# Streamed high and low parts in one tile, in pieces of 64 or 128 bytes, and another order in one down projection

## The chip, the cores and the metric

The kernel runs on one core of a Trainium2 chip. The metric is device microseconds of one execution. TensorE has two levels of clock, 1.2 and 2.4 GHz; the profile shows the granted share of the higher one.

## The reference

Two blocks run one after the other on 256 tokens of width 1024, each of two layers, and what they compute is float32. The first block's layers have four branches (a convolution, a sparse attention, a chunked linear recurrence and a memory attention) and a feed forward. The second block's layers are modulated: a vector `c` gives shift, scale and gate for each half of a layer. Its layer 0 mixes with two chunked recurrences, its layer 1 with a long convolution. Both end in the feed forward that the change touches:

```
h = h + g2 * swiglu(modulate(h, norm2_w[i], sh2, sc2), ffn_w1[i], ffn_w3[i], ffn_w2[i])
swiglu(u, w1, w3, w2) = (silu(u @ w1) * (u @ w3)) @ w2          # 1024 -> 2816 -> 1024
modulate(x, gain, shift, scale) = rmsnorm(x, gain) * (1 + scale) + shift
```

A last norm follows.

## The kernel before

Activations lie transposed: channels on the 128 partitions, `KT` = 8 tiles of channels, and the 256 tokens along the row. A product in float32 accuracy is made of three matmuls in the format float32r: the weights `w` are split into a high part `wh` and what is left over, `wl`, and so is the streamed operand (`xh` and `xl`, in other stages `hh` and `hl`, `ph` and `pl`, `ydh` and `ydl`). `mm3` (lines 486 to 490) issues high by high, then high weights by the low operand, then low weights by the high operand, all into one place of PSUM. The weights are the stationary operand, 128x128 at a time; the activations are streamed, 256 columns.

`weights` (line 458) brings a unit of four tiles of rows by 256 columns, 512 KB, by a DMA on SP's queue; ScalarE writes `wh` (line 474), VectorE writes `wl` (line 475). There are 4 buffers of `w` and 3 each of `wh` and `wl`. A unit feeds 24 matmuls: 4 row tiles, 2 halves of 128 columns, 3 products. `s_tiles` (line 492) runs through the row tiles for one output of 2 x 128 channels by 256 tokens.

`ffn` (line 540) loops over 11 blocks of 256 hidden channels: a gate product and an up product, SiLU on ScalarE, a multiplication on VectorE, and `split` (line 455) into `ph` and `pl`, two tiles of 22 rows of 256 floats. Then come four down projections over the 22 rows, and `residual` adds them to `xT`. `ffn2` (line 1984) prepares it in the second block: `ahead` and `ffn_ahead` run the first hidden block on a not yet normalised copy (`uh`, `ul`), while `norm_split` (line 437) writes `xh` and `xl`, two tiles of 8 rows of 256 floats under the tags `hh` and `hl` of the layer's pool. In layer 0 the tiles `uh` and `ul` lie at the other end of SBUF than in layer 1. The order of the work on each engine is that of the program text. The first block calls `ffn` as well, without `gcol`.

Of the kernel before, what the change touches and what calls it, by code (L numbers as in the profile page):

```python
# [11 lines left out]
F32R = mybir.dt.float32r  # L12
# [7 lines left out]
S = 256  # L20
KT = 8
# [4 lines left out]
FT = FFN // 128  # L26
# [212 lines left out]
class Halves:  # L239


    def __init__(self, *tiles):
        self.tiles = tiles

    def __getitem__(self, i):
        return self.tiles[i[1] // 4][i[0], i[1] % 4, i[2]]


class Ahead:
    def __init__(self, h, l, n, pb, lp):  # L250
        self.h, self.l, self.n, self.pb, self.lp = h, l, n, pb, lp
# [2 lines left out]
class K:  # L254
    def __init__(self, tc, A, out, tap=None):
        self.tc, self.nc, self.A, self.out, self.tap_ = tc, tc.nc, A, out, tap
        self.es = ExitStack()
        self.bank, self.mmbank = "aux", "mm"
        self.held = None
        self.bg, self.rate, self.due, self.has_modc, self.fg = None, 0.0, 0.0, False, iter(())  # L260
        es = self.es
        self.const = es.enter_context(tc.tile_pool(name="const", bufs=1))
        self.xp = es.enter_context(tc.tile_pool(name="xp", bufs=1))
        self.wp = es.enter_context(tc.tile_pool(name="wp", bufs=2))
        self.wpool, self.wb = self.wp, WB
        self.ps = es.enter_context(tc.tile_pool(name="ps", bufs=4, space=bass.MemoryType.PSUM))
        self.wk = es.enter_context(tc.tile_pool(name="wk", bufs=2))
        self.dr = es.enter_context(tc.tile_pool(name="dr", bufs=1, space=bass.MemoryType.DRAM))
# [168 lines left out]
    def norm_split(self, src, g, hh, hl, shift=None, r=None, bank="aux2", u=None):  # L437
        nc = self.nc
        pb = u.pb if u else self.rstd_bcast(src, r, bank)
        for k in range(KT):  # L440
            t = self.wk.tile([128, S], F32, tag="nt", bufs=3, name="nt")
            nc.vector.scalar_tensor_tensor(t, src[:, k, :], g[:, k:k + 1], pb, op0=OP.mult, op1=OP.mult)
            if shift is None:
                nc.scalar.copy(hh[:, k, :], t)
                nc.vector.tensor_tensor(hl[:, k, :], t, hh[:, k, :], OP.subtract)
            else:
                nc.scalar.activation(hh[:, k, :], t, AF.Identity, bias=shift[:, k:k + 1])
                nc.vector.scalar_tensor_tensor(hl[:, k, :], t, shift[:, k:k + 1], hh[:, k, :], op0=OP.add,
                                               op1=OP.subtract)
# [3 lines left out]
        self.nc.vector.scalar_tensor_tensor(lo, src, g, hi, op0=OP.mult, op1=OP.subtract)  # L453

    def split(self, src, hi, lo):
        self.nc.scalar.copy(hi, src)
        self.nc.vector.tensor_tensor(lo, src, hi, OP.subtract)

# [26 lines left out]

    def mm3(self, ps, wh, wl, xh, xl, start, stop):
        nc = self.nc
        nc.tensor.matmul(ps, wh, xh, start=start, stop=False)  # L488
        nc.tensor.matmul(ps, wh, xl, start=False, stop=False)  # L489
        nc.tensor.matmul(ps, wl, xh, start=False, stop=stop)  # L490

    def s_tiles(self, ps, at, xh, xl, kt=KT, first=True, last=True, x0=0, mws=((0, 128), (128, 128)), k0=0):

        for n in range(kt):
            k = (n + k0) % kt
            wh, wl = at(k)
            st, sp = first and n == 0, last and n == kt - 1  # L500
            for i, (m0, mw) in enumerate(mws):
                self.mm3(ps[:mw, i * S:(i + 1) * S], wh[:, m0:m0 + mw], wl[:, m0:m0 + mw], xh[:, x0 + k, :],
                         xl[:, x0 + k, :], st and i == 0, sp and i == len(mws) - 1)

    def s_form(self, name, l, c0, ncols, xh, xl, kt=KT, k0=0):
# [31 lines left out]
        nc.vector.tensor_tensor(pr, pg, pu, OP.mult)  # L537
        return pr

    def ffn(self, xh, xl, l, w_gate, w_up, u0, w_down, gcol=None, first=None, scale=None):  # L540
        nc = self.nc
        with self.pool("ffn") as fp:
            ph = fp.tile([128, FT, S], F32R, name="ph")
            pl = fp.tile([128, FT, S], F32R, name="pl")
            for i in range(FFN // 256):
                self.pump()
                if i == 0 and first is not None:
                    prv = first
                else:
                    pg = self.mm()  # L550
                    self.s_tiles(pg, self.weights(w_gate, l, i * 256), xh, xl)
                    pu = self.mm()
                    self.s_tiles(pu, self.weights(w_up, l, u0 + i * 256), xh, xl)
                    sg = fp.tile([128, 512], F32, tag="f1", bufs=2, name="f1")
                    pr = fp.tile([128, 512], F32, tag="f2", bufs=2, name="f2")
                    if scale is not None:
                        for o, ps in ((sg, pg), (pr, pu)):
                            nc.vector.tensor_tensor(o.rearrange("p (m t) -> p m t", m=2),
                                                    ps.rearrange("p (m t) -> p m t", m=2),
                                                    scale[:, None, :].to_broadcast([128, 2, S]), OP.mult)  # L560
                        pg, pu = sg, pr
                    nc.scalar.activation(sg, pg, AF.Silu)
                    nc.vector.tensor_tensor(pr, sg, pu, OP.mult)
                    prv = pr.rearrange("p (m t) -> p m t", m=2)
                self.split(prv, ph[:, 2 * i:2 * i + 2, :], pl[:, 2 * i:2 * i + 2, :])
            self.rate = RATES[4]
            for i in range(4):
                self.pump()
                pd = self.mm()
                self.s_tiles(pd, self.weights(w_down, l, i * 256, FT), ph, pl, FT)  # L570
                for m in range(2):
                    self.residual(2 * i + m, pd[:, m * S:(m + 1) * S], gcol)

    def residual(self, k, ps, gcol=None):
        nc = self.nc
        if gcol is None:
            nc.vector.tensor_tensor(self.xT[:, k, :], self.xT[:, k, :], ps, OP.add)
        else:
            nc.vector.scalar_tensor_tensor(self.xT[:, k, :], ps, gcol[:, k:k + 1], self.xT[:, k, :], op0=OP.mult,
                                           op1=OP.add)  # L580
# [1402 lines left out]

    def ffn2(self, i, hp, fp=None):
        A = self.A
        xh = hp.tile([128, KT, S], F32R, tag="hh", name="xh")
        xl = hp.tile([128, KT, S], F32R, tag="hl", name="xl")
        g, sh = self.gains[:, 2 * i + 1, :], self.mod[i][:, 24:32]
        with self.pool("f2") as lp:
            with self.pool("f2u", None if i else "right") as up:  # L1990
                u = self.ahead(self.xT, g, up, sh)
                self.norm_ahead(u, self.xT)
                pr = self.ffn_ahead(u, i, "ffn_w1_2", "ffn_w3_2", 0, lp)
                self.norm_split(self.xT, g, xh, xl, shift=sh, u=u)
            self.fill(9, "aux2")
            if fp:
                self.dft_loads()
            self.ffn(xh, xl, i, "ffn_w1_2", "ffn_w3_2", 0, "ffn_w2_2", gcol=self.mod[i][:, 40:48], first=pr)
        self.tap(f"hl{i}", self.xT)


# [280 lines left out]
```

## Time and profile before

| | us |
|---|---|
| median of 3 runs | 2015.56 (2011.5 to 2017.99) |
| the profiled execution | 2005.55 |
| its span, first to last instruction | 2003.8 |
| PE busy | 1950.2 |
| DVE busy | 1487.3 |
| ACT busy | 1049.6 |
| mean granted clock of TensorE | 0.981 |

PE is TensorE's matmuls and PEld its weight loads; DVE is VectorE, ACT ScalarE, SP the engine that issues the DMAs. The length of a matmul in the profile is from its start to its modelled end; matmuls follow one another before the one in front has ended, so the distance of two starts, and not the length, is what one costs. The count of a stretch holds every instruction that lies in it, if only in part, so a stretch of 25 us with matmuls of 0.28 us holds the starts of 25.28 us.

### The profile page before, as it was taken

To read this page: it belongs to the slowest core of one execution; us is meant where nothing else is said; L and a number is where in the kernel's file an instruction comes from. 1 tells how busy PE (TensorE), PEld (TensorE's weight loads), DVE (VectorE), ACT (ScalarE), POOL (GpSimd) and SP (SyncE) were. 2 spreads that over 40 slices of the span, in tenths; PEclk is the share of its full clock that TensorE was granted. 3 is DMA by queue.
4 is the path that set the end of the run, shared out by engine and by line. 5 is a ranking of instruction groups with operands and counts; after the bars stand their busy time and mean duration, and the time that the engine had idled before them with its cause. 6 is when DMAs were issued, how large, how long until landed. Compare 5 with 4: busy or idle time off the path is not lost.

```text
span 2003.8 us, 39753 instructions
## 1 busy us (share of the span) xinstructions
PE 1950.2 (97%) x16274; PEld 1889.9 (94%) x16274; DVE 1487.3 (74%) x2374; ACT 1049.6 (52%) x1640; POOL 96.4 (5%) x86
## 2 busy tenths in 40 slices
PE   8999999999999999999979999999999999999998
PEld 8999999999999999999969999998899999999998
DVE  5988877796776879968657775777776556897554
ACT  6663454675544673454544544645345445656443
POOL 0001000010000000000100000000020000001001
PEclk9999999999999999999987999989999999999999
DMA  8865756875667756748523456534246666546663
GB/s 317 280 217 170 232 179 209 292 256 192 205 221 242 244 188 220 242 129 288 180 89 101 153 166 192 175 99 124 85 124 181 192 189 219 162 126 187 192 188 126
DMA packets 118558, 379.55 MB, mean 189 GB/s; under 512 B 18239, under 2 KB 28776, under 8 KB 117096
## 3 DMA queue, kind: packets, MB, share of 16 engines
q1 hardware_dynamic: 118376, 377.02, 58.2%
q8 instruction: 127, 2.08, 0.4%
q14 instruction: 55, 0.45, 0.1%
HBM read 366.53 MB, written 10.25 MB: 188 GB/s over the span
## 4 chain that ended last, share of the span: by engine, by line
PE 88%; DVE 4%; ACT 3%; issue 2%; DMA 2%; POOL 0%; SPq 0%; DVEq 0%; POOLq 0%; ACTq 0%
PE mm L490 23%; PE mm L488 23%; PE mm L489 23%; DVE wl L475 2%; ACT wh L474 1%; PE aux L1230 1%; PE mm L524 1%; PE mm L525 1%; PE mm L526 1%; PE mm L2080 1%; PE aux L2132 1%; PE aux L490 1%; PE aux L2115 1%; PE aux L861 1%; PE aux L488 1%
## 5 line engine op out<-in xcount | busy, mean ns | idle before, releaser
L474 ACT CAST wh<-w 128x1024 fp32r<-128x1024 f32 (+2 forms) x570 | 588.9, 1035 | 644.7 <-PE mm L489 485.3
L475 DVE TENSOR_TENSOR wl<-w,wh 128x1024 fp32r<-128x1024 f32 (+2 forms) x570 | 684.6, 1203 | 302.1 <-ACT wh L474 298.6
L488 PE MATMUL mm<-hh,wh 128*128 128x256 f32 x1776 | 502.7, 283 | 2.3 <-ACT bq L768 2.0
L490 PE MATMUL mm<-hh,wl 128*128 128x256 f32 (+1 forms) x1776 | 503.0, 283 | 1.1 <-DVE wl L475 1.1
L489 PE MATMUL mm<-hl,wh 128*128 128x256 f32 x1776 | 501.2, 282 | 0.0
L488 PEld LDWEIGHTS mm<-hh,wh 128*128 128x128 f32 x1776 | 335.2, 189 | 6.1 <-ACT bq L768 2.4
L490 PEld LDWEIGHTS mm<-hh,wl 128*128 128x128 f32 (+1 forms) x1776 | 334.9, 189 | 3.7 <-issue 1.5
L489 PEld LDWEIGHTS mm<-hl,wh 128*128 128x128 f32 x1776 | 335.1, 189 | 3.0 <-issue 2.3
L490 PE MATMUL mm<-xh,wl 128*128 128x256 f32 x960 | 270.6, 283 | 1.6 <-DVE wl L475 1.5
L488 PE MATMUL mm<-xh,wh 128*128 128x256 f32 x960 | 269.4, 282 | 2.1 <-DVE dqT L1268 1.1
L489 PE MATMUL mm<-xl,wh 128*128 128x256 f32 x960 | 269.6, 283 | 0.2
L490 PE MATMUL mm<-ph,wl 128*128 128x256 f32 x704 | 196.1, 279 | 0.0
L488 PE MATMUL mm<-ph,wh 128*128 128x256 f32 x704 | 195.8, 278 | 0.0
L489 PE MATMUL mm<-pl,wh 128*128 128x256 f32 x704 | 195.7, 278 | 0.0
L488 PEld LDWEIGHTS mm<-xh,wh 128*128 128x128 f32 x960 | 182.4, 190 | 6.1 <-issue 2.9
L490 PEld LDWEIGHTS mm<-xh,wl 128*128 128x128 f32 x960 | 182.7, 190 | 5.6 <-issue 3.0
L489 PEld LDWEIGHTS mm<-xl,wh 128*128 128x128 f32 x960 | 182.2, 190 | 2.9 <-issue 2.2
L1224 DVE SCALAR_TENSOR_TENSOR macc<-mw,cs,macc 128x512 f32<-128x512 f32 x196 | 145.5, 747 | 11.9 <-DMA mw<-in_t_mod_w 11.4
L489 PEld LDWEIGHTS mm<-pl,wh 128*128 128x128 f32 x704 | 132.4, 188 | 0.0
L490 PEld LDWEIGHTS mm<-ph,wl 128*128 128x128 f32 x704 | 132.1, 188 | 0.0
L488 PEld LDWEIGHTS mm<-ph,wh 128*128 128x128 f32 x704 | 132.0, 188 | 0.0
L488 PE MATMUL mm<-brh,wh 128*128 128x256 f32 x384 | 107.8, 281 | 0.0
(702 smaller groups left out, 3518.7 us busy)
## 6 DMA issues: line engine op xcount, KB each, us to landing
w<-in_t_w_in SPq DMA_DIRECT2D x148, 512.0 KB, 4.2
w<-in_t_ffn_w SPq DMA_DIRECT2D x128, 512.0 KB, 3.7
mw<-in_t_mod_w SPq DMA_DIRECT2D x96, 512.0 KB, 4.8
w<-in_t_ffn_w_up SPq DMA_DIRECT2D x88, 512.0 KB, 3.5
w<-in_t_ab_w_in SPq DMA_DIRECT2D x42, 512.0 KB, 3.4
w<-in_t_ffn_w_down SPq DMA_DIRECT2D x40, 512.0 KB, 3.6
w<-in_t_w_lift SPq DMA_DIRECT2D x32, 512.0 KB, 3.9
w<-in_t_hy_w_in SPq DMA_DIRECT2D x24, 512.0 KB, 3.7
```

Of the source, the lines that this page charges most:

```text
L474: nc.scalar.copy(wh, w)
L475: nc.vector.tensor_tensor(wl, w, wh, OP.subtract)
L488: nc.tensor.matmul(ps, wh, xh, start=start, stop=False)
L489: nc.tensor.matmul(ps, wh, xl, start=False, stop=False)
L490: nc.tensor.matmul(ps, wl, xh, start=False, stop=stop)
L524: nc.tensor.matmul(o, h, wh, start=(k + tb == 0), stop=False)
L525: nc.tensor.matmul(o, h, wl, start=False, stop=False)
L526: nc.tensor.matmul(o, l, wh, start=False, stop=(k == KT - 1 and tb == 1))
L861: nc.tensor.matmul(ps[:, jj * S:jj * S + ns], qr[r, 2 * jp + jj, tb * 128:(tb + 1) * 128], kr[r, 0, :ns], start=True, stop=True)
L1224: nc.vector.scalar_tensor_tensor(acc, v[:, k, :], sc, acc, op0=OP.mult, op1=OP.add)
L1230: nc.tensor.matmul(ps[:, m:m + 1], acc[:, m * 128:(m + 1) * 128], self.ones[:, :1], start=True, stop=True)
L2080: nc.tensor.matmul(ps[:, i * 256:(i + 1) * 256], self.Hm[:, (2 * j + i) * 128:(2 * j + i + 1) * 128], t[:, j, :], start=True, stop=True)
```

## The change

The second block's feed forwards get one tile `xx` in place of `xh` and `xl`. In each of its 8 rows the high and the low part take turns in pieces: 16 floats (64 bytes) in layer 0, 32 floats (128 bytes) in layer 1. A view, `Lines`, picks the high or the low pieces, so that a matmul streams 256 floats as 16 pieces with a step of 128 bytes, or as 8 pieces with a step of 256. `like` gives the other operands of an instruction the same shape. In layer 1 `ph` and `pl` share a tile `pp` in the same way, in pieces of 64 bytes. In layer 0 they stay two tiles, and the three matmuls of a step of the down projection come in another order: low weights by the high operand, then high by high, then high weights by the low operand. `xx` is a tile of the pool `f2`, not of the layer's pool.

```diff
+class Lines:
+    def __init__(self, tile, j):
+        self.tile, self.j = tile, j
+
+    def __getitem__(self, i):
+        return self.tile[i[0], i[1], :, self.j, :]
+
+def like(src, dst):
+    if len(dst.shape) == len(src.shape):
+        return src
+    lead = "p m" if len(src.shape) == 3 else "p"
+    return src.rearrange(f"{lead} (a b) -> {lead} a b", b=dst.shape[-1])
...
@@ norm_split, with a shift
+                t = like(t, hh[:, k, :])
@@ split
+        src = like(src, hi)
@@ mm3
-        nc.tensor.matmul(ps, wh, xh, start=start, stop=False)
-        nc.tensor.matmul(ps, wh, xl, start=False, stop=False)
-        nc.tensor.matmul(ps, wl, xh, start=False, stop=stop)
+        order = [(wl, xh), (wh, xh), (wh, xl)] if self.low_first else [(wh, xh), (wh, xl), (wl, xh)]
+        for i, (w, x) in enumerate(order):
+            nc.tensor.matmul(ps, w, x, start=start and i == 0, stop=stop and i == 2)
@@ s_tiles
+                h = xh[:, x0 + k, :]
+                self.mm3(like(ps[:mw, i * S:(i + 1) * S], h), wh[:, m0:m0 + mw], wl[:, m0:m0 + mw], h,
@@ ffn(..., lines=None)
+            if lines:
+                pp = fp.tile([128, FT, S // lines, 2, lines], F32R, name="pp")
+                ph, pl = Lines(pp, 0), Lines(pp, 1)
...
+            self.low_first = gcol is not None and not lines
             for i in range(4):
...
+            self.low_first = False
@@ ffn2
-        xh = hp.tile([128, KT, S], F32R, tag="hh", name="xh")
-        xl = hp.tile([128, KT, S], F32R, tag="hl", name="xl")
...
+            xx = lp.tile([128, KT, 8 if i else 16, 2, 32 if i else 16], F32R, name="xx")
+            xh, xl = Lines(xx, 0), Lines(xx, 1)
...
+            self.ffn(xh, xl, i, "ffn_w1_2", "ffn_w3_2", 0, "ffn_w2_2", gcol=self.mod[i][:, 40:48], first=pr,
+                     lines=16 if i else None)
```

## Rows read from the trace of the kernel before

**Rows 1.** The page's head: busy time by engine, and shares of the chain.
```profile
PE 1950.2 (97%) x16274; PEld 1889.9 (94%) x16274; DVE 1487.3 (74%) x2374; ACT 1049.6 (52%) x1640; POOL 96.4 (5%) x86
...
PE 88%; DVE 4%; ACT 3%; issue 2%; DMA 2%; POOL 0%; SPq 0%; DVEq 0%; POOLq 0%; ACTq 0%
PE mm L490 23%; PE mm L488 23%; PE mm L489 23%; DVE wl L475 2%; ACT wh L474 1%; PE aux L1230 1%; PE mm L524 1%; PE mm L525 1%; PE mm L526 1%; PE mm L2080 1%; PE aux L2132 1%; PE aux L490 1%; PE aux L2115 1%; PE aux L861 1%; PE aux L488 1%
```
**Rows 2.** Stretches: PE, PEld, DVE, ACT, POOL busy (count); clock, DMA share, GB/s.
```profile
1200.00:1225.00 25.00, 25.00 (x215) 25.00 (x214) 13.97 (x16) 10.75 (x14) 0.82 (x1) 1.00 0.66 211
...
1575.00:1600.00 25.00, 25.00 (x223) 25.00 (x222) 14.30 (x15) 12.02 (x15) 0.00 (x0) 1.00 0.69 193
...
1950.00:1975.00 25.00, 25.00 (x219) 25.00 (x218) 13.31 (x16) 10.36 (x12) 2.85 (x3) 1.00 0.64 201
```
**Rows 3.** Order of time, PE, layer 0's gate and up: start us, length.
```profile
1559.73 0.28 PE L488 MATMUL mm<-xh,wh 128*128 128x256 f32 x1
...
1560.07 0.28 PE L488 MATMUL mm<-xh,wh 128*128 128x256 f32 x1
1560.18 0.28 PE L489 MATMUL mm<-xl,wh 128*128 128x256 f32 x1
...
1562.79 0.28 PE L488 MATMUL mm<-xh,wh 128*128 128x256 f32 x1
```
**Rows 4.** Order of time, PE, first block's feed forward.
```profile
560.02 0.28 PE L488 MATMUL mm<-hh,wh 128*128 128x256 f32 x1
...
562.85 0.28 PE L488 MATMUL mm<-hh,wh 128*128 128x256 f32 x1
```
**Rows 5.** Order of time, PE, layer 0's output projection.
```profile
1490.81 0.28 PE L488 MATMUL mm<-ydh,wh 128*128 128x256 f32 x1
...
1493.31 0.28 PE L488 MATMUL mm<-ydh,wh 128*128 128x256 f32 x1
```
**Rows 6.** Order of time, PE, first block, another stage.
```profile
354.60 0.28 PE L488 MATMUL mm<-hh,wh 128*128 128x256 f32 x1
...
357.32 0.28 PE L488 MATMUL mm<-hh,wh 128*128 128x256 f32 x1
```
**Rows 7.** Order of time, PE, layer 1's down projection.
```profile
1965.12 0.28 PE L488 MATMUL mm<-ph,wh 128*128 128x256 f32 x1
...
1967.95 0.28 PE L488 MATMUL mm<-ph,wh 128*128 128x256 f32 x1
```
**Rows 8.** Order of time, weight loads, the stretch of rows 3.
```profile
1560.07 0.19 PEld L489 LDWEIGHTS mm<-xl,wh 128*128 128x128 f32 x1
```
**Rows 9.** Order of time, matmuls and weight loads with shorter streams, merged.
```profile
1729.45 3.29 PE L2132 MATMUL aux<-G,hy 128*128 128x128 f32 x28
...
197.71 0.74 PEld L1230 LDWEIGHTS aux<-cst,macc 128*128 128x128 f32 x6
```
**Rows 10.** Groups, 1505 to 1690 us: busy us, mean ns, idle before them.
```profile
L489 PE MATMUL mm<-xl,wh 128*128 128x256 f32 x320 | 87.9, 276 | 0.0
L474 ACT CAST wh<-w 128x1024 fp32r<-128x1024 f32 (+1 forms) x68 | 69.7, 1027 | 85.5 <-PE mm L489 68.1 <-issue 16.8 <-ACT sq L366 0.4
L490 PEld LDWEIGHTS mm<-xh,wl 128*128 128x128 f32 x320 | 60.1, 188 | 0.4 <-DVE wl L475 0.3
L490 PE MATMUL mm<-ph,wl 128*128 128x256 f32 x176 | 48.6, 276 | 0.0
```
**Rows 11.** Order of time, transposes, merged.
```profile
1734.47 0.60 PE L2106 MATMUL aux<-cst,hsd 128*128 128x128 f32 x4
```
**Rows 12.** Lines 1724 and 1725: least, median, greatest ns, starts, forms.
```profile
L1724 PE MATMUL aux<-dX,dG x256: 219/219/293, 1126.5 to 1396.3; 64*64 64x32 f32 x128
...
L1725 ACT COPY dT<-aux x8: 353/372/372, 1129.9 to 1396.7; 128x256 f32<-128x256 f32 x8
```
**Rows 13.** Tile xh, 1505 to 1690 us: the same columns, then who waited.
```profile
L447 ACT ACTIVATE xh<-nt,mod x8: 492/500/513, 1507.2 to 1518.2; 128x256 fp32r<-128x256 f32 x8
...
  PEld mm L488: 0.3, 1
```

More of the change, by code (lines that the diff above doesn't have):

```diff
@@ L258, in __init__ @@
         self.bank, self.mmbank = "aux", "mm"
-        self.held = None
+        self.held, self.low_first = None, False
         self.bg, self.rate, self.due, self.has_modc, self.fg = None, 0.0, 0.0, False, iter(())
@@ L501, in s_tiles @@
             for i, (m0, mw) in enumerate(mws):
-                self.mm3(ps[:mw, i * S:(i + 1) * S], wh[:, m0:m0 + mw], wl[:, m0:m0 + mw], xh[:, x0 + k, :],
+                h = xh[:, x0 + k, :]
+                self.mm3(like(ps[:mw, i * S:(i + 1) * S], h), wh[:, m0:m0 + mw], wl[:, m0:m0 + mw], h,
                          xl[:, x0 + k, :], st and i == 0, sp and i == len(mws) - 1)
@@ L538, in ffn_ahead, with ffn @@
         return pr
-    def ffn(self, xh, xl, l, w_gate, w_up, u0, w_down, gcol=None, first=None, scale=None):
+    def ffn(self, xh, xl, l, w_gate, w_up, u0, w_down, gcol=None, first=None, scale=None, lines=None):
         nc = self.nc
         with self.pool("ffn") as fp:
-            ph = fp.tile([128, FT, S], F32R, name="ph")
-            pl = fp.tile([128, FT, S], F32R, name="pl")
+            if lines:
+                pp = fp.tile([128, FT, S // lines, 2, lines], F32R, name="pp")
+                ph, pl = Lines(pp, 0), Lines(pp, 1)
+            else:
+                ph = fp.tile([128, FT, S], F32R, name="ph")
+                pl = fp.tile([128, FT, S], F32R, name="pl")
             for i in range(FFN // 256):
@@ L1997, in ffn2 @@
                 self.dft_loads()
-            self.ffn(xh, xl, i, "ffn_w1_2", "ffn_w3_2", 0, "ffn_w2_2", gcol=self.mod[i][:, 40:48], first=pr)
+            self.ffn(xh, xl, i, "ffn_w1_2", "ffn_w3_2", 0, "ffn_w2_2", gcol=self.mod[i][:, 40:48], first=pr,
+                     lines=16 if i else None)
         self.tap(f"hl{i}", self.xT)
```

## The prediction

> **What bounds the kernel now.** I read the head of the page first. TensorE is busy for 1950.2 of 2003.8 us, and the chain of waits that ended last is 88% PE; its three largest shares are the three matmul lines of `mm3` [rows 1]. So the end is set by how often a matmul can start, and a changed wait on another engine matters only where it leaves a gap on PE. The second view is the table of stretches [rows 2], for the stages that the diff touches: layer 0's second feed forward (about 1510 to 1680 us) and layer 1's (about 1822 to 1993). PE is busy in all of each 25 us there, at a granted clock of 1.00: nothing to win from waits, nor from the clock. What differs is the count: 223 matmuls in a stretch of these stages, 215 in the first block's feed forward at the same busy share and clock.
>
> The third view, the order of time, shows why. In layer 0's gate and up part, 27 matmuls lie between the starts at 1559.73 and 1562.79: 113.3 ns each [rows 3]. In the first block 24 lie between 560.02 and 562.85: 117.9 ns each [rows 4]. With operand `ydh` 21 lie between 1490.81 and 1493.31: 119.0 ns [rows 5]. The shape is the same in all three, 256 fp32 columns against 128x128 weights. What differs is where the streamed tile lies. By the program's own addresses each weight row starts 128 bytes behind a multiple of 256; `xh`, `xl` and the second block's `ph`, `pl` start 64 behind one, `hh` and `hl` 192, `ydh` 128, just where the weights do. So the price of a matmul hangs on the streamed tile's place against the weights, and that is what the change moves. It is not place alone: `hh` at its usual place also ran at 113.3 ns for a while (24 from 354.60 to 357.32 [rows 6]), and `ph` of layer 1, usually at 113.3, slipped to 117.9 (24 from 1965.12 to 1967.95 [rows 7]). There are levels, and a stage can fall from one to another; the stretch with the slip counts 219 instead of 223 [rows 2].
>
> What the time goes into: a weight load starts just behind a matmul, and the next matmul only when that load is through (a matmul at 1560.07, the load for the next at 1560.07 too, the next at 1560.18 [rows 3, 8]). The loop is a loop of weight loads. Matmuls with a stream half as long and weights as wide give its floor: 28 in 3.29 us, less 0.27 for the last one's own length, are 27 intervals of 111.9 ns; six weight loads whose matmuls stream one column take 0.74 us, less 0.19, five of 110 ns [rows 9]. Against 111.9 the stages lose 1.4 ns a matmul now, which I read as the two reads of SBUF getting in each other's way. This reading is a theory; no row shows a bank.
>
> A rule of the Trainium skill speaks against it and against the change: "SBUF — State Buffer", section "A bandwidth-pool intuition that's wrong", gives the weight load a second, independent read port, so a stream's layout should cost nothing. By that the sum would be 0. The trace disagrees with it: 113.3, 117.9 and 119.0 ns for one shape.
>
> **The change part by part.**
>
> Gate and up, both layers: 10 pairs of tiles at 2 x 8 x 2 x 3 = 96 matmuls are 960 in each layer (three lines with 320 [rows 10]). The streamed row becomes pieces of 64 bytes (layer 0) or 128 (layer 1), high and low in turn. The count of matmuls stays. The second down projection (3 x 176 = 528) gets pieces of 64. Together 2448 matmuls stream pieces. What one costs then no row shows, as no matmul of 256 columns streams pieces. Below: 111.9 ns, the loop of weight loads [rows 9], gains 1.4 x 2448 = 3.4 us. Lower still: transposes, where four in 0.60 us less 0.27 are 109 to 110 ns each [rows 11], would gain 4.0 x 2448 = 9.8 us. Above: 119.0 ns [rows 5] loses 5.7 x 2448 = 14.0 us. I take 111.9: each part now touches only every other piece of a line, so the weights' row meets it in half of its places, and the nearest rows for a load with little in its way are those of rows 9. That is a gain of 3.4 us.
>
> That pieces in themselves cost no stream time is bounded by one row: line 1724's matmuls stream two pieces of 16 elements in one half of the calls and 32 in one run in the other, and all 256 have 219 ns as least and median [rows 12]. This is a tile of 32 columns, too short to show a nanosecond a piece; 16 pieces at 1 ns would give 16 ns on a stream, and nothing covers this but the few ns by which the weight loads are longer. It belongs to the slow end.
>
> The slip in layer 1's down projection [rows 7] costs 4 matmuls of 113.3 ns in its stretch, 219 for 223 [rows 2], or 0.45 us; with what falls into the next stretch, which holds the kernel's end too, I put it at 0.6 us. If the new layout does not slip, that goes. If both down projections slipped throughout, 1056 x 4.5 = 4.8 us would come. I take the gain of 0.6.
>
> Low weights first, layer 0's down projection (528 matmuls, tiles plain as before): the three matmuls of a step are the same three, and each load still runs beside a stream at the same distance: high beside weights twice, low once. I cost it at nothing. Two covers are needed. The first matmul of a unit now waits for `wl` (DVE) where it waited for `wh` (ACT). In steady state both are written more than a unit ahead: ACT's casts wait 68.1 us in all for PE to give back a buffer, and PE waits 0.3 us for `wl` over that feed forward [rows 10]. And `wh` is given back by the third matmul and not by the second, 0.11 us later; 22 units x 0.11 = 2.5 us if ACT had no such idle time. Bounds: -0.8 us (528 at 111.9) to +2.5.
>
> Writing in pieces: 8 ACT instructions of 500 ns [rows 13] and as many of DVE's write a layer's `xx`, 10 or 11 of each kind write `pp`. The nearest row is an ACT copy of 128x256 that writes runs of 16 or 32 floats, 353 to 372 ns [rows 12]; no penalty is seen. The pieces matter where PE waits for the norm: 0.3 us for `xh` [rows 13]. If each of these 16 were 0.1 us longer and all on the path, both layers would lose 3.2 us; I take 0.
>
> Moved tiles: `xx` is a tile of its own below `f0`, 16 KB, so `ph` moves by 16 KB: the same place modulo 256 for the plain pair of layer 0. No DMA, no queue and no instruction before 1490 us moves, so the weights arrive as before; the DMA engines are 0.64 to 0.69 busy in these stretches [rows 2].
>
> **Sum.** -3.4 - 0.6 = -4.0 us on the profiled execution of 2005.55 (span 2003.8, 1.75 us around it): 2001.5. That execution lies 10 us below the median of the three runs, 2015.56, and below the lowest of them, 2011.5; I take the difference over to the median: 2011.5.
>
> **The rivals.**
>
> B, the loads too get out of the way: the loop falls below the 111.9 ns, to the 109.3 of the transposes [rows 11]; -9.8 - 0.6, 2005.2. For it: the weights in a transpose are 128 wide too. Against it: no plain matmul in the rows goes below 111.9 in a long run. The Trainium skill has a rule that would give this: "TensorE: Matmul & The Clock Gate", section "Back-to-back issue gap", estimates 256/2.4 + 2.5 = 109.2 ns; by it 4.1 x 2448 = 10.0 us would go. The trace's long runs of this shape do not show it.
>
> C, nothing happens: the level of 113.3 is the same for pieces, since half as many meetings that last twice as long cost the same; 2015.6. For it: three tiles at the same place, `xh` and `ph` of both layers, all have 113.3 whatever lies beside them. Against it: the level does respond to place.
>
> D, slower: in 64-byte pieces the low part starts 64 bytes behind the high, at 128 modulo 256, just where the weights start, as `ydh` does now. Where the start decides, the low matmuls go to 119.0: a third of 960 + 528, 496 x 5.7 = 2.8 us; in 128-byte pieces the low part starts at 192, the place of `hh`: 320 x 4.6 = 1.5. That is +4.3, 2019.9. It decides as soon as place of start, and not the run of lines, sets the level. If the whole triple falls with its low member, which is how the slips look (all three at 117.9), it is 1488 x 5.7 + 960 x 4.6 = +12.9, 2028.5. For it: rows 4 and 5 are just these places. Against it: rows 6, the same place at 113.3.
>
> **How the numbers follow.** About 0.3% (6 us) is what a measurement of this kernel can tell from no change. Chances: the forecast 0.48, B 0.19, C 0.14, D 0.19. The forecast's own range is 2006 to 2017, by run-to-run spread and by the bounds of low-first and of the slips. Faster by over 0.3%, below 2009.5: nearly all of B (0.18) and two fifths of the forecast (0.20), 0.38. Slower, above 2021.6: most of D, 0.17. Within: the rest, 0.45. The range runs from 2001, B with its spread, to 2023, which takes in D by starts alone and leaves its worse form out.
>
> **What would show it.** Right: 226 or so matmuls in a stretch of gate and up (25.28 us, with the ends, by 111.9 ns), both layers alike; 223 still in layer 0's down projection; no 219 in layer 1's. B shows 230. C shows 223 everywhere. D shows 215 to 219 with pieces, and layer 0, with 64 bytes, worse than layer 1. Writing in pieces shows as longer ACT and DVE rows for `xx` and more PE idle ahead of the first tile. The prediction is wrong if the stretches keep their count, or if the total moves by much more than 2448 times the change of one interval.

## The result, and the profile after

The changed kernel is slower by half a per cent: a ratio of 1.0051, with a 95% interval of 1.0038 to 1.0065. Its median is 2022.97 us (2010.81 to 2027.54, 19 runs) beside 2012.73 us (2006.05 to 2017.99, 19 runs) for the kernel before; worked out from the ratio's interval, the loss is 7.6 to 13.1 us. The forecast was a gain of 4.0 us, 2011.5 us by the median known then.

The profiled execution after took 2022.28 us, with a span of 2020.5, 16.7 more than the span before. The head of its page and the shares of its chain of waits, to be held against [rows 1]:

```profile
PE 1967.4 (97%) x16274; PEld 1907.2 (94%) x16274; DVE 1488.1 (74%) x2374; ACT 1049.4 (52%) x1640; POOL 96.2 (5%) x86
...
PE 85%; DVE 5%; ACT 4%; issue 3%; DMA 2%; POOL 0%; SPq 0%; DVEq 0%; POOLq 0%; ACTq 0%
```

The same number of instructions on every engine; VectorE and ScalarE are as busy as before to 1 us; TensorE is busy for 17.2 us more and stands idle no longer than before (53.1 us of the span, 53.6 before). So the matmuls have become dearer, and TensorE waits no longer for the others. The stretches say where. This is the view of [rows 2], with the same columns (PE, PEld, DVE, ACT, POOL busy and count; clock, DMA share, GB/s):

```profile
1200.00:1225.00 25.00, 25.00 (x214) 25.00 (x214) 14.16 (x16) 10.94 (x15) 0.82 (x1) 1.00 0.67 209
...
1575.00:1600.00 25.00, 25.00 (x210) 25.00 (x209) 13.43 (x13) 11.21 (x13) 0.00 (x0) 1.00 0.64 186
1640.00:1665.00 25.00, 25.00 (x223) 25.00 (x222) 15.52 (x18) 12.93 (x18) 2.82 (x3) 1.00 0.62 192
1860.00:1885.00 25.00, 25.00 (x210) 25.00 (x210) 13.60 (x13) 11.30 (x14) 0.00 (x0) 1.00 0.58 187
1950.00:1975.00 25.00, 25.00 (x210) 25.00 (x209) 12.13 (x14) 9.39 (x11) 1.20 (x1) 1.00 0.63 186
```

Where pieces are streamed, 210 matmuls fit into 25 us instead of 223 or 219: layer 0's gate and up (1575), layer 1's gate and up (1860), layer 1's down projection (1950). Layer 0's down projection (1640), with plain tiles and low weights first, has 223 as before, and the first block (1200) has 214 for its 215. Busy share and granted clock are full in all of these stretches. The order of time in layer 0 (start us, length, engine, line, tiles), to be held against [rows 3]:

```profile
1559.33 0.28 PE L510 MATMUL mm<-xx,wl 128*128 128x256 f32 x1
1559.44 0.40 PE L510 MATMUL mm<-xx,wh 128*128 128x256 f32 x2
...
1562.94 0.28 PE L510 MATMUL mm<-xx,wl 128*128 128x256 f32 x1
```

From `wl` to `wl` are ten times three matmuls: 3.61 us by 30 is 120.3 ns, where it was 113.3. Over all rows in pieces the mean from start to start is 120.3 ns (some 2,430 intervals, the few above 135 ns left out), and for the same matmuls before 113.7. 6.6 ns times 2448 is 16.2 us. The spans differ by 16.7, but that the two agree so closely is luck in part: 2.5 us of the 16.7 lie ahead of layer 0's second feed forward, which started at 1509.8 us before and at 1512.3 after. From that start to the end the two profiles have 494.0 and 508.2 us, 14.2 more. Writing in pieces costs nothing; the rows for tile `xx` (least, median, greatest ns) stand beside [rows 13], 502 ns as median for 500:

```profile
L466 ACT ACTIVATE xx<-nt,mod x8: 492/502/509, 1509.8 to 1520.8; 128x256 fp32r<-128x256 f32 x8
L467 DVE SCALAR_TENSOR_TENSOR xx<-nt,mod,xx x8: 473/476/484, 1510.6 to 1522.2; 128x256 fp32r<-128x256 f32 x8
```

### The profile page after: what moved, and what is told of

Read it like the earlier page. It is cut to its first block, busy times and chain, and to the rows that moved or that the text cites. A ratio compares the mean times of both kernels' runs of the same rounds, so it can differ in the third digit from the quotient of the medians.

```text
span 2020.5 us, 39753 instructions
## 1 busy us (share of the span) xinstructions
PE 1967.4 (97%) x16274; PEld 1907.2 (94%) x16274; DVE 1488.1 (74%) x2374; ACT 1049.4 (52%) x1640; POOL 96.2 (5%) x86
## 4 chain that ended last, share of the span: by engine, by line
PE 85%; DVE 5%; ACT 4%; issue 3%; DMA 2%; POOL 0%; SPq 0%; DVEq 0%; POOLq 0%; ACTq 0%
PE mm L510 66%; PE aux L510 2%; DVE wl L495 2%; ACT wh L494 1%; PE aux L1257 1%; DMA mw<-in_t_mod_w 1%; DVE macc L1251 1%; PE mm L545 1%; PE mm L546 1%; PE mm L547 1%; PE aux L2160 1%; PE aux L2143 1%; PE aux L888 1%; PE aux L1670 1%; PE aux L853 1%
## 5 line engine op out<-in xcount | busy, mean ns | idle before, releaser
L510 PE MATMUL mm<-xx,wh 128*128 128x256 f32 x1280 | 231.6, 283 | 0.6 <-ACT uc L443 0.5
L510 PEld LDWEIGHTS mm<-xx,wh 128*128 128x128 f32 x1280 | 198.0, 188 | 1.1 <-ACT uc L443 0.7
L510 PE MATMUL mm<-xx,wl 128*128 128x256 f32 x640 | 181.5, 284 | 0.2 <-DVE wl L495 0.2
L510 PE MATMUL mm<-ph,wl 128*128 128x256 f32 x528 | 147.0, 278 | 0.0
L510 PE MATMUL mm<-ph,wh 128*128 128x256 f32 x528 | 146.9, 278 | 0.0
L510 PE MATMUL mm<-pl,wh 128*128 128x256 f32 x528 | 146.7, 278 | 0.0
L510 PEld LDWEIGHTS mm<-xx,wl 128*128 128x128 f32 x640 | 120.4, 188 | 0.6 <-DVE wl L495 0.6
L510 PE MATMUL mm<-brh,wl 128*128 128x256 f32 x384 | 107.2, 280 | 0.0
L510 PE MATMUL mm<-brl,wh 128*128 128x256 f32 x384 | 107.2, 280 | 0.0
L510 PEld LDWEIGHTS mm<-pl,wh 128*128 128x128 f32 x528 | 99.1, 188 | 0.0
```

The lines of the kernel that those rows point to most:

```text
L510: nc.tensor.matmul(ps, w, x, start=start and i == 0, stop=stop and i == 2)
```

## The experiments

The question was why a streamed row in pieces costs 120 ns. The theories: by place against the weights' row (P), by the breaks, or jumps, themselves (J), or not by the pieces at all but by the shared tile (T). "Place" is where a row starts behind a multiple of 256 bytes.

**Halves.** The changed kernel: the shared tile, its place and the order stay; the pieces go.

```diff
-xx = lp.tile([128, KT, 8 if i else 16, 2, 32 if i else 16], F32R, name="xx")
+xx = lp.tile([128, KT, 1, 2, 256], F32R, name="xx")
-     lines=16 if i else None)
+     lines=256 if i else None)
```

> The changed kernel with one edit: high and low parts still share a tile, in the same places and with the same low weights first, but each row is two unbroken halves of 1,024 bytes. Three theories of why a matmul of the changed parts starts every 120.4 ns on the mean instead of every 113.3. Pieces by place (P): a streamed row costs by where in a line of 256 bytes it lies against the weights' row (unbroken rows of the kernel before: 113.3 at 64, 117.9 at 192, 119 to 120 at 128, where the weights' rows start), and pieces of 64 or 128 bytes put every row partly in the bad places. P expects 113.3 ns in layer 0's gate and up projections and 113.3 to 114.3 in layer 1, 222 to 226 matmuls per 25 us there, and a time like the kernel before's, 0.3 to 0.7% below the changed kernel's. Jumps (J): each break in a streamed row costs stream time, wherever it lies. J expects the same of this run as P. Shared tile (T): it is that the parts share a tile or where that tile is put, not the pieces. T expects 120 ns and 210 per 25 us still, and the changed kernel's time.

Measured: 2007.55 us (2002.76 to 2010.25, 11 runs), 0.9996 of the kernel before run beside it (0.9985 to 1.0007). The stretches are those of the kernel before:

```profile
1575.00:1600.00 25.00, 25.00 (x223) 25.00 (x222) 13.81 (x14) 11.97 (x14) 0.00 (x0) 1.00 0.60 190
...
1860.00:1885.00 25.00, 25.00 (x223) 25.00 (x222) 14.82 (x16) 12.01 (x14) 0.00 (x0) 1.00 0.65 197
1950.00:1975.00 25.00, 25.00 (x220) 25.00 (x219) 15.51 (x19) 11.74 (x14) 3.48 (x3) 1.00 0.61 191
```

T falls. The pieces are the cause of the loss; the shared tile and its place are worth nothing either way.

**Longer pieces.** The changed kernel with 256 bytes in layer 0's rows and layer 1's hidden rows, 512 in layer 1's normalized rows.

```diff
-xx = lp.tile([128, KT, 8 if i else 16, 2, 32 if i else 16], F32R, name="xx")
+xx = lp.tile([128, KT, 2 if i else 4, 2, 128 if i else 64], F32R, name="xx")
-     lines=16 if i else None)
+     lines=64 if i else None)
```

> The changed kernel with longer pieces: 256 bytes in layer 0's normalized rows and in layer 1's hidden rows, 512 bytes in layer 1's normalized rows; nothing else differs. The start of every piece is then at the same place in a line of 256 bytes as in an unbroken row, but the row still jumps 3 times (once with 512 bytes). P expects 113.3 ns in layer 0's gate and up projections, as in an unbroken row at place 64, and 113.3 to 117.8 in layer 1. J with a price per jump: 15 jumps and 7 jumps both cost about 7 ns in the changed kernel, so a jump costs 0.5 to 1.0 ns, and 3 jumps give 114.7 to 116.3, one jump 113.8 to 114.3. J as a step (any break costs the whole): 120. T expects 120.

Measured in one run: 2007.57 us (the kernel before beside it has a median of 2006.91), and the stretches at 1575 (256 bytes) and 1860 (512 bytes):

```profile
1575.00:1600.00 25.00, 25.00 (x223) 25.00 (x222) 13.61 (x13) 12.19 (x15) 0.00 (x0) 1.00 0.64 193
...
1860.00:1885.00 25.00, 25.00 (x223) 25.00 (x223) 14.51 (x15) 11.49 (x13) 0.00 (x0) 1.00 0.64 197
```

These rows jump three times and once, and cost nothing. A fixed price per jump (114.7 to 116.3 ns expected) and a step for any break (120) both fall; P stands at this point.

**Moved tiles.** The changed kernel with unbroken halves, and a pad in front of `xx`, which moves layer 0's streamed rows to place 128 of a line of 256 bytes and layer 1's to 192.

```diff
+lp.tile([128, 32 if i else 16], F32, name="xpad")
-xx = lp.tile([128, KT, 8 if i else 16, 2, 32 if i else 16], F32R, name="xx")
+xx = lp.tile([128, KT, 1, 2, 256], F32R, name="xx")
-     lines=16 if i else None)
+     lines=256 if i else None)
```

> No pieces at all: unbroken halves in the shared tile as in the first run, but a pad moves the tiles of layer 0's second feed forward by 64 bytes (its rows start at place 128 of a line of 256 bytes, where the weights' rows start) and those of layer 1's by 128 bytes (place 192). P expects 119 to 120 ns in layer 0's gate and up and down projections (215 or fewer per 25 us) and 117.8 in layer 1 (with slips to 113.3 possible, as the kernel before shows at 192), so about the changed kernel's loss, 10 to 20 us of span, with no piece in it. J expects 113.3 in both layers, and the time of the kernel before. T expects 120 in the gate and up projections and 113.3 in layer 0's down projection, whose tiles are not shared.

Measured in one run: 2010.89 us, and

```profile
1575.00:1600.00 25.00, 25.00 (x211) 25.00 (x210) 13.70 (x14) 11.05 (x13) 0.00 (x0) 1.00 0.59 183
1640.00:1665.00 25.00, 25.00 (x210) 25.00 (x209) 12.90 (x14) 10.10 (x13) 1.94 (x2) 1.00 0.58 191
1860.00:1885.00 25.00, 25.00 (x215) 25.00 (x214) 13.73 (x15) 11.48 (x13) 0.00 (x0) 1.00 0.60 182
```

Without a piece, place 128 gives 210 or 211 in both parts of layer 0, and place 192 gives 215. So the place of an unbroken row does set its price, as the prediction read it from [rows 3 to 5]. It is layer 0 that shows this: 215 is a count that place 64 can have too, as a second profile below shows. J, which expects 113.3 in both layers, falls as a full account. (The single time shows less than the stretches do, as layer 0's feed forward began 7 us earlier in this profile than in the first one of the kernel before. From that start to the end it is 506.5 us, 12.5 more than the 494.0 before.) Place and breaks had to be parted by measuring each alone.

**A series.** 48 matmuls of each of 43 kinds, in the pattern of `mm3`, run twice; the kernel runs the series and then only the final norm.

```diff
+todo += [(f"w128x{xp}p{p}h", dict(wp=128, xp=xp, p=p, step=2 * p, lo=p))
+         for p in (16, 32, 64, 128) for xp in (0, 64, 128, 192)]
...
+    series(t, **d)
...
-K(tc, aps, out[0]).run()
+K(tc, aps, out[0]).run(stages=())
```

> A series of its own: it loads the input, runs 46 kinds of series of 48 f32r matmuls (the second time in reverse order) in the kernel's pattern (high weights by high and by low operand, low weights by high), and leaves the whole model out but the final norm. Kinds: unbroken rows of 256 columns at places 0, 64, 128 and 192 with weights at place 128 and at place 0; pieces of 64, 128, 256 and 512 bytes at the four places; pieces of 64 bytes with 256 bytes from start to start; stationary operands of 64 and of 32 columns, whose load is short; and rows of 512 columns. P expects unbroken rows with weights at 128: 113.3 at 64, 117.8 at 192, 119 to 120 at 128; with weights at 0 the same list turned by 128 (113.3 at 192, 119 to 120 at 0); pieces of 256 and 512 bytes like unbroken ones at the same place; pieces of 64 bytes with 256 between starts 113.3 at the good places; and with 32 stationary columns no difference between pieces and unbroken rows, because a short load leaves nothing to collide with. J expects pieces of 64 bytes dearer than unbroken rows at every place, also with 32 stationary columns, and twice as much dearer with 512 columns; and unbroken rows the same at every place.

The order of time of the first pass; a row holds 48 matmuls, so its length, less 0.28 for the last one's own (0.27 with 240 columns), divided by 47 is the time from start to start, good to 0.3 ns. In a name, `w` is the weights' place, `x` the stream's, `p` the floats in a piece, `s` the floats from start to start (twice `p` where none stands), a `c` or `p512` an unbroken row; `quarter` has 32 stationary columns.

```profile
47.94 5.86 PE L2252 MATMUL w128x0c<-big,w 128*128 128x256 f32 x48
53.63 5.61 PE L2252 MATMUL w128x64c<-big,w 128*128 128x256 f32 x48
59.09 5.90 PE L2252 MATMUL w128x128c<-big,w 128*128 128x256 f32 x48
64.83 5.82 PE L2252 MATMUL w128x192c<-big,w 128*128 128x256 f32 x48
...
87.58 5.63 PE L2252 MATMUL w0x192c<-big,w 128*128 128x256 f32 x48
...
98.86 5.94 PE L2252 MATMUL w128x64p16h<-big,w 128*128 128x256 f32 x48
...
121.98 5.93 PE L2252 MATMUL w128x64p32h<-big,w 128*128 128x256 f32 x48
...
145.02 5.62 PE L2252 MATMUL w128x64p64h<-big,w 128*128 128x256 f32 x48
...
190.29 5.93 PE L2252 MATMUL w128x64p16s64h<-big,w 128*128 128x256 f32 x48
...
241.92 5.92 PE L2252 MATMUL quarterx64p16h<-big,w 128*32 128x256 f32 x48
...
253.38 5.89 PE L2252 MATMUL quarterx64p32h<-big,w 128*32 128x256 f32 x48
...
264.84 5.62 PE L2252 MATMUL quarterx64p512h<-big,w 128*32 128x256 f32 x48
270.29 5.61 PE L2252 MATMUL quarterx128p512h<-big,w 128*32 128x256 f32 x48
```

Unbroken rows: 118.7, 113.4, 119.6 and 117.9 ns at places 0, 64, 128 and 192 with the weights at 128; with the weights at 0 the cheap place is 192 (113.8). With 128 stationary columns what counts is the distance: 64 bytes ahead of the weights' start, modulo 256, is cheap. J's "same at every place" falls. Pieces: 120.4 (64 bytes) and 120.2 (128 bytes) at the place where unbroken rows have 113.4, and 119.8 to 121.3 at the other three and in the second pass. Pieces of 256 bytes: 113.6 at place 64. So far P; but two of its predictions fall. Pieces of 64 bytes that all start at place 64 (256 bytes from start to start) have 120.2, not 113.3. And with 32 stationary columns, where places 64 and 128 are alike (113.6 and 113.4), pieces still cost 120.0 and 119.4. Breaking the row costs time by itself, with a short weight load (0.108 us in the trace with 32 stationary columns) as with a long one (0.188 with 128). Since the pieces of 64 bytes that all start at place 64 are dear as well, it is not the start of the low part at a bad place either. How the place acts depends on the load's length too: with 64 stationary columns unbroken rows had 118.9 ns at place 64 and 113.8 at 128 (116.7 in the second pass), the other way round than with 128.

The Trainium skill, "SBUF — State Buffer", section "Specifications (TRN2)", gives lines of 16 bytes and a penalty for each line newly touched. By that a row in pieces of 64 bytes, which touches no more such lines than an unbroken one, would cost nothing; the series does not agree, with 6 to 7 ns.

**A second series**, on what makes a broken row dear.

```diff
+todo += [(t + "c", d), (t + "outgap16h", dict(d, op=(16, 32)))]
+todo += [(f"{t}p{p}s{st}h", dict(d, p=p, step=st))
...
+todo += [(f"{t}n240p{p}s{st}h", dict(d, p=p, step=st, cols=240))
```

> A second series of its own (the model left out but the final norm), 48 matmuls of each kind, twice. What makes a broken row slow? Length (L): a row is slow, about 120 ns, as soon as its pieces are shorter than 256 bytes, whatever the gap. Crossing (C): what counts is how many more lines of 256 bytes the row touches than an unbroken one, so that pieces of 64 or 128 bytes with gaps of 16 bytes, and pieces of 240 bytes that start every 256, cost little over the unbroken row (113.5 to 115). Jumps (J): a price for each jump, so pieces of 32 bytes (31 jumps) are dearer than pieces of 64 (15 jumps) by as much as those are over the unbroken row: 126 or more. All with 128 and with 32 stationary columns; with 32 the place should not matter. Rows of 240 columns in pieces of 160, 192 and 240 bytes against an unbroken one of 240: L expects all three slow by 6 ns, C the last one fast. Output in pieces of 64 bytes with a gap, input unbroken: 113.7 if the cost is the reading's. Rows of 512 columns with 32 stationary columns: unbroken 227 at every place, pieces 238 (a price per column) or 233 (a price per matmul). Unbroken rows at 16 places 16 bytes apart with weights at 128: 113.7 at 64 and 117 to 120 at 0, 128 and 192; in between unknown, expected between the neighbours or dearer.

In the names, `full` has 128 stationary columns and `quarter` 32; `n240` streams 240 columns, `wide` 512; `outgap` has the output in pieces and the stream unbroken; `place` is followed by the place of an unbroken row.

```profile
132.17 5.60 PE L2254 MATMUL place240c<-big,w 128*128 128x256 f32 x48
137.61 5.61 PE L2254 MATMUL fullc<-big,w 128*128 128x256 f32 x48
143.06 5.60 PE L2254 MATMUL fulloutgap16h<-big,w 128*128 128x256 f32 x48
148.50 5.84 PE L2254 MATMUL fullp8s16h<-big,w 128*128 128x256 f32 x48
154.18 5.93 PE L2254 MATMUL fullp16s20h<-big,w 128*128 128x256 f32 x48
...
188.59 5.92 PE L2254 MATMUL fullp64s96h<-big,w 128*128 128x256 f32 x48
194.35 5.61 PE L2254 MATMUL fullp64s128h<-big,w 128*128 128x256 f32 x48
199.80 5.91 PE L2254 MATMUL fullp128s144h<-big,w 128*128 128x256 f32 x48
...
221.72 5.54 PE L2254 MATMUL fulln240p512s512h<-big,w 128*128 128x240 f32 x48
...
294.71 5.54 PE L2254 MATMUL quartern240p40s64h<-big,w 128*32 128x240 f32 x48
300.08 5.41 PE L2254 MATMUL quartern240p48s64h<-big,w 128*32 128x240 f32 x48
305.33 5.36 PE L2254 MATMUL quartern240p60s64h<-big,w 128*32 128x240 f32 x48
310.52 5.28 PE L2254 MATMUL quartern240p512s512h<-big,w 128*32 128x240 f32 x48
...
326.73 11.28 PE L2254 MATMUL widex64p512s512h<-big,w 128*32 128x512 f32 x48
...
360.07 11.78 PE L2254 MATMUL widex64p16s32h<-big,w 128*32 128x512 f32 x48
371.69 11.47 PE L2254 MATMUL widex64p32s64h<-big,w 128*32 128x512 f32 x48
```

None of the three theories comes through. Crossing falls: a gap of 16 bytes behind every 64 costs all of it (120.2). Jumps fall: pieces of 32 bytes, with twice the jumps, have 118.3. Length holds for short pieces, with a slope: pieces of 160, 192 and 240 bytes, 256 from start to start, cost 5.5, 2.8 and 1.7 ns over the unbroken 106.6 with 32 stationary columns (with 128, where the unbroken row has 112.1, only the shortest costs something in both passes, 1.3 ns). But length is not all: pieces of 256 and of 512 bytes whose starts fall on different places modulo 256 (`p64s96`, `p128s144`) have 120.0 and 119.8, and those that all start at one place (`p64s128`) 113.4 (117.9 in the second pass, of which more below). With 32 stationary columns pieces of 256 bytes with gaps of 16 or 64 bytes lie between, at 115.6. With 512 columns and 32 stationary ones pieces of 64 bytes cost 0.50 us by 47, 10.6 ns, over the unbroken row and pieces of 128 bytes 4.0, where 256 columns pay some 6 to 7 for either: the price grows with the columns for the one and not for the other. (With 128 stationary columns the first series had 5.3 and 4.5 for 512 columns, so there it grows for neither.) An output in pieces costs nothing (113.2). What holds for all rows of 256 columns at place 64 in both series, with 128 or 32 stationary columns: a row has a cheap level where it is unbroken, or where its pieces are of 256 bytes or more and all start at one place modulo 256. The mechanism behind that stays open.

**The order alone.** The kernel before, with only the low weights first in layer 0's down projection.

```diff
-nc.tensor.matmul(ps, wh, xh, start=start, stop=False)
...
+order = [(wl, xh), (wh, xh), (wh, xl)] if self.low_first else [(wh, xh), (wh, xl), (wl, xh)]
+self.low_first = gcol is not None and l == 0
```

> The kernel before with one part of the change alone: layer 0's down projection takes the low weights first; no shared tile, no pieces. In the profile of the changed kernel this projection's 528 matmuls took 113.37 ns on the mean against 113.33 before. Theory: the order costs and gives nothing; 528 matmuls at 113.3 to 113.4 ns, a ratio of 1.000 within 0.002. Rival: it gives back some of what the pieces cost (a first load of low weights that are ready later would show as a wait at each of the four groups, 0.1 to 2 us in all, dearer; or the matmul that follows a group's end finds its weights loaded, cheaper by as much).

Measured: 2007.11 us (2002.26 to 2012.18, 12 runs), 0.9996 (0.998 to 1.0011). The order is worth nothing that these runs can tell.

**Second profiles** of both kernels, unedited, because the medians differ by less than the profiles.

> The kernel before once more, unedited, for a second profile of it. Open is why the profiles differ by 16.7 us of span and the medians by 10.2. Theory S: unbroken rows at place 64 have two levels, 113.3 and 117.8 ns, and which of them a stretch takes differs from one execution to the next (rows of the same place had 113.9 in the first profile of the kernel before, 114.5 with halves, 115.3 in the two runs with the first block moved), while short pieces always take 120: so the loss is 2,448 times (120.4 less 113.5 to 117.8). S expects the second feed forwards' unbroken rows in this profile anywhere from 113.4 to 116, and a span that goes with it. Rival E: the difference of medians holds something the change gives back elsewhere; E expects the same 113.9 and 1950 us of TensorE's busy time as in the first profile.

> The changed kernel once more, unedited, for a second profile of it. S (see the run of the kernel before) expects the rows in pieces at 120.4 ns within 0.5 again, with no second level, and differences to the first profile only in stages whose rows are unbroken. E expects the same profile as the first.

Stretches of the kernel before, second profile, then one of the run of the order alone, then of the changed kernel, second profile:

```profile
750.00:755.00 5.00, 5.00 (x29) 5.00 (x28) 4.10 (x9) 0.53 (x2) 0.94 (x1) 0.57 0.57 183
...
1400.00:1490.00 90.00, 84.24 (x623) 76.62 (x622) 71.00 (x142) 34.62 (x82) 12.94 (x15) 0.98 0.34 106
...
1575.00:1600.00 25.00, 25.00 (x215) 25.00 (x214) 13.61 (x13) 11.03 (x14) 0.00 (x0) 1.00 0.59 189
1640.00:1665.00 25.00, 25.00 (x215) 25.00 (x214) 13.39 (x16) 11.79 (x16) 1.94 (x2) 1.00 0.59 184
1860.00:1885.00 25.00, 25.00 (x223) 25.00 (x222) 14.18 (x14) 11.51 (x13) 0.00 (x0) 1.00 0.65 198
```

```profile
1400.00:1490.00 90.00, 85.38 (x616) 75.42 (x615) 59.74 (x128) 28.85 (x70) 8.64 (x10) 0.91 0.27 87
```

```profile
1575.00:1600.00 25.00, 25.00 (x209) 25.00 (x209) 13.10 (x13) 11.96 (x14) 0.00 (x0) 1.00 0.62 180
...
1860.00:1885.00 25.00, 25.00 (x211) 25.00 (x210) 13.61 (x13) 10.93 (x13) 0.00 (x0) 1.00 0.63 187
```

The same unbroken rows at the same place, in the same program, counted 223 at 1575 in the first profile [rows 2] and 215 in the second: place 64 has two levels, and a whole feed forward can run on either (layer 0's ran on the dear one here, layer 1's gate and up, at 1860, on the cheap one). Pieces have 120.3 ns in both profiles of the changed kernel. So the loss is 2448 x (120.3 - 113.7) = 16.2 us against the first profile of the kernel before and 2448 x (120.3 - 115.4) = 12.0 against the second. In the second, layer 0's plain down projection ran on the dear level as well (215 at 1640), and in both profiles of the changed kernel on the cheap one, which gives 528 x 4.4 = 2.3 us back and leaves 9.7. From the start of layer 0's second feed forward to the end the second profiles have 499.1 and 508.0 us, 8.9 more, where the first ones had 14.2. The measured 7.6 to 13.1 takes in the lower loss. S expected these rows and levels; E, which expected 113.9 ns again, falls, although TensorE's busy time came out as it said (1949.3 us).

It is not the whole spread, and the span did not go with the rows as S expected: the second profile's span, 2000.6, is shorter than the first's in spite of its dearer rows, because the start of layer 0's feed forward wanders by 14 us, from 1501.5 to 1515.8, over profiles of kernels that are the same up to there. The clock has a part in that: over 1400 to 1490 us the granted clock was 0.98 in the profile with the earliest start, the second of the kernel before, and 0.91 in one with the latest, the run of the order alone. When it falls differs as well: at 750 us it is 0.57 in the second profile, mostly the level of 1.2 GHz, and 1.00, that of 2.4 GHz, in the first. TensorE counts as busy throughout ahead of that fall, but from 744.71 to 747.04 us it had started 20 matmuls that stream one or two columns; the first profile has the same 20, 0.8 us later, and no fall. What decides it is open.

**The rule put to use.** The series says that the first block's rows, at place 192, lie badly. One number moves them to 64, another to 0: from 24 to 56 floats are 128 bytes more, and from 24 to 40 are 64, and 192 + 64 is a multiple of 256. The expectation for the second run took that place for 128, which is wrong.

```diff
-rp.tile([128, 24], F32, name="rpad")
+rp.tile([128, 56], F32, name="rpad")
```

> The kernel before with one number changed: the pad ahead of the first block's tiles is 56 floats long instead of 24, so that the first block's streamed rows (normalized rows, branch rows, hidden rows) start at place 64 of a line of 256 bytes instead of 192; no piece, no shared tile, no other edit. The place theory as the series left it (unbroken rows, weights at 128: 113.7 ns at 64, 117.8 at 192) expects the 7,300 or so matmuls of the first block that now take 116.6 to 118.0 ns to take 113.5: summed over their rows in the trace of before 27 us less, 1.3%, some 222 to 226 matmuls per 25 us in the first block's feed forwards where there were 215, and a time near 1982. The rival that the level is a matter of history (the same place 192 shows 113.3 in some stretches and 117.9 in others) and that something else sets the first block's rate expects no change over 0.3%.

> The kernel before with the pad ahead of the first block's tiles 40 floats long instead of 24: the same streamed rows of the first block at place 128, where the weights' rows start. The place theory (120 ns at 128 in the series and in the run with moved tiles, 116.6 to 118.0 ns at 192 before) expects 7,300 matmuls dearer by 2.0 to 3.4 ns, 15 to 25 us more, 0.7 to 1.2%, a time near 2027, and 208 to 210 matmuls per 25 us in the first block's feed forwards. The rival of history expects no change over 0.3%.

The edit of the second run has 40 in place of 56. Measured at 64: 1998.33 us (1991.98 to 2010.11, 12 runs), 0.9949 (0.9926 to 0.9972) of the kernel before run beside it, the fastest version here by that ratio. At 0: 2019.59 us (2012.7 to 2030.56, 10 runs), 1.0052 (1.002 to 1.0084), by the ratio 10.5 us more. The 15 to 25 us expected were those of place 128, which this run does not have. What the series has for place 0, 118.7 ns, fits its time: the first block's intervals rose from 117.3 to 118.8 ns on the mean, 10 us over some 7,180 of them. The rival of history expected no change over 0.3%; the near ends of the two 95% intervals lie inside that, so it is the matmuls' intervals that speak against it. The stretch at 1200, which has 215 in [rows 2], at 64 and with it another feed forward, and then at 0 (at 560, where 215 were counted before, the run at 0 has 214):

```profile
1200.00:1225.00 25.00, 25.00 (x223) 25.00 (x222) 16.17 (x19) 13.01 (x19) 2.69 (x3) 1.00 0.60 185
...
1860.00:1885.00 25.00, 25.00 (x215) 25.00 (x214) 13.45 (x13) 11.96 (x14) 0.00 (x0) 1.00 0.65 187
```

```profile
1200.00:1225.00 25.00, 25.00 (x210) 25.00 (x210) 14.74 (x17) 10.66 (x13) 0.00 (x0) 1.00 0.75 226
```

At 64 the gain is 0.5% and not the 1.3% expected. Of the 27 us, 19 came in the matmuls of the profiled run: the first block's 7,180 intervals fell from 117.3 to 114.7 ns on the mean, and not to 113.5, as some stretches run on the level of 117.8 at place 64 too. And layer 1's second feed forward, which the edit leaves alone, ran on that level in this profile (215 at 1860). Of the 19 us, 12.3 show as an earlier start of layer 0's second feed forward, and 3.4 were lost again behind it; where the rest went was not followed up. The two levels are a limit on what placing can give.

## Why the prediction was wrong

- What bounds the kernel: right. The end is set by how often a matmul can start: from the start of layer 0's second feed forward on, the first pair of profiles differs by 14.2 us and the second by 8.9, where the matmuls' intervals sum to 16.2 and 9.7.
- Price of a matmul by the streamed tile's place: right, and shown by the moved tiles and by the series. That two reads meet stays a theory. For it: with the short load of 32 stationary columns the two places tried are alike. Not explained by it: unbroken rows with that short load have a dear level too, 113.3 ns in the first pass of the second series and 116.6 in the second.
- Price in pieces, the term of 111.9 ns (-3.4 us): this is the step that failed, in sign. It took from the meeting of reads that a row that touches half of each line meets the weights half as often, and took a broken row for as cheap to stream as an unbroken one. It measured 120.3, 1.3 ns above the upper bound of 119.0, because a broken row costs 6 ns even where no long weight load stands against it; that is 16.2 us in the place of -3.4. Why a broken row costs this is open. The floor of 111.9 was not one for 256 columns either: the second series has 113.4 with 32 stationary columns as with 128. Nor do [rows 3, 8] show a matmul that starts only when its load is through: the load that starts at 1560.07 is recorded for 0.19 us, to 1560.26, and its matmul starts at 1560.18.
- The row that bounded this at nothing, [rows 12], could not: it streams 32 columns. The prediction said so, put 16 ns beside it, and did not let either into the sum or into a rival of its own. That was the rival to have: "pieces cost stream time", for which the trace had no row against it.
- Rival D had the sign, for another reason. By it the high parts keep 113.3 ns and only the low ones go to 119.0, +4.3 us. Its worse form, the whole triple dear, +12.9, comes near what was measured, but by luck: it goes by where the parts start, and pieces that all start at the good place have 120.2 as well. The measured median, 2022.97, lies just inside the stated range, at the end that was there for D. By operand, 64-byte rows have 119.2 for the high part and 121.4 for the low by the high weights, and 128-byte rows 119.5 for both. Its sign of layer 0 being worse than layer 1 hardly showed: 210 in both gate and up parts, 120.5 and 120.0 ns.
- Rivals B and C: no stretch of 230, and none of 223 with pieces. Both wrong.
- The slip, -0.6 us: there is none with pieces (210 at 1950), and no run shows a cheap level of theirs to slip from. The two levels of unbroken rows, treated there as a small matter of one stretch, are 4.4 ns a matmul on a whole feed forward.
- Low weights first, 0: right, 0.9996. Writes in pieces, 0: right, 502 ns for 500. Moved tiles, 0: right by the run with halves.

The Trainium skill's rule that the prediction weighed, a second, independent read port for the weight load ("SBUF — State Buffer", section "A bandwidth-pool intuition that's wrong (but worth ruling out)"), would have given 0 here by the prediction's reading, that a stream's layout then costs nothing. The series does not agree with that reading at 128 stationary columns (113.4 to 119.6 ns by place); at 32, with 113.6 and 113.4 at the two places tried, it does for the place, and with 120.0 for pieces of 64 bytes it does not.

## What to carry to other kernels

A streamed operand belongs in unbroken rows, or in pieces of 256 bytes or more that all start at one place modulo 256; 64- or 128-byte pieces cost this kernel 4 to 6% of every such matmul. Where a kernel is a loop of matmuls with a weight load each, lay the streamed tiles so that they start 64 bytes ahead of the weights' rows modulo 256: a pad of a few floats was worth 0.5% here. That holds for 256 float32r columns against 128x128 weights; with 64 stationary columns place 64 was the dear one of the two tried. And where a prediction rests on a shape that no row shows, that shape's worst price belongs among the rivals.

## What the hardware showed that was not expected

- A matmul of 256 columns has 113.4 ns as its floor with 32 stationary columns as with 128, so the 113.3 of [rows 3] does not come from the length of the load, and the loop of weight loads (111.9, [rows 9]) lies below it: these rows leave no 1.4 ns to win. The loop shows with 240 columns: 112.1 ns with 128 stationary columns, 106.6 with 32.
- Of 16 places 16 bytes apart, two are cheap with the weights at 128: 64 (113.6 ns) and 240 (113.2, and 114.9 in the second pass); the rest have 116.6 to 120.
- The level of one place can change with nothing but the execution: 113.4 or 117.7 ns for the same 1,488 matmuls of layer 0 in two profiles of one program.
